# Keys and queries, and gates and first products, through joint scratch tensors and joint loads; another rhythm of the odd operand sums; seven more filler matmuls at the start

## The chip, the cores and the metric

One core of a Trainium2 chip runs the kernel. The time is the device time of one execution in microseconds (us), as the median of several. The engines are PE (matmul), PEld (PE's weight loads), DVE (VectorE), ACT (ScalarE), POOL (GpSimd) and SP (SyncE, which here only issues transfers). SPq and ACTq are the rows in which SP and ACT issue transfers.

## The reference, cut to what matters

A residual block over x of 2048 rows by 1024 columns, in float32:

```
h      = rms_norm(x) * (1 + scale(c)) + shift(c)
x_rnn, z_rnn, q, k, v, z_attn, g_r, g_a = split(h @ W_in)          # 8 x 1024 columns
y_rnn  = (rg_lru(conv(x_rnn)) * silu(z_rnn)) @ w_out_rnn
y_attn = (mixture over windows 128/1, 512/4, 2048/16 of attention(rope(q), rope(k), v)
          * silu(z_attn)) @ w_out_attn                              # 8 heads of 128
merged = sigmoid(g_r + bg_r) * y_rnn + sigmoid(g_a + bg_a) * y_attn
out    = rms_norm(x + gate(c) * (merged @ w_o))
```

The keys and values of the three windows are taken at strides 1, 4 and 16.

## The kernel before, in words

Every float32 operand is split in a high part of type fp32r (on ACT, line 159) and a low remainder (on DVE, line 168, or POOL, line 165). A product is then three matmuls for each 128 rows of its contraction (mm3, line 151), each with a 128x512 moving operand. The 2048 rows are four banks of 512 columns once transposed; the kernel's first half (f = 0) treats banks 0 and 1, its second half (f = 1) banks 2 and 3.

**The start** (lines 640 to 830). The modulation by c is computed column by column: sums on DVE (`sums`, line 669), column sums over the partitions on PE (`columns`, one-column matmuls into V), `modulation` on DVE (L692, L693), and then `build_x`, which makes the operand of a 128-row block k: ACT writes its high part T (L570) and a full copy hf (L573), DVE the remainder (L168). The first products X, Z, W, V need it. ACT also splits the raw weights, S<-R (`hi_k`, L159), which come by transfer as R<-in_w_in; these splits stand in ACT's order between the builds. Between the column sums PE runs filler matmuls (`idle_matmuls`, lines 625 to 633: bf16, 128x512, into a tile that nobody reads); their counts stand in lines 768 to 779 as written out by hand.

**The input projection** multiplies 2x2 blocks of operands by sums and differences of weights, seven products for eight (a Strassen form). The operands of an odd bank and the sums T1 to T4 are made by the generator `build_odd` (line 592): four yields build the odd bank's blocks (hx), then eight more parts, two for each k, make the sums. A part takes DVE operations L609 to L619 and, for each result, a split: T<-hx or T<-t on ACT, the remainder on DVE. `values_half` (line 877) says when each part is issued beside the value products: "free" (its operations take their place in the order as they come), "tied" (`tc.issue_after(last_ev[0])`: behind the last eviction so far), or one by one beside the last four quarter products. The eviction of a value product is ACT's ev<-X (L855), after which PE may write that bank again.

**Scratch.** Queries and keys are written transposed to DRAM tensors qT and kT, for each class c (row number modulo 4) 512 columns of 128 per bank. The gates of the two branches are in grT and gaT, the first projection's gated result in mrT.

**Attention and the output projections** run together from about 1340 us on: the head's work in units, and between them steps of `steps` (line 1723), a generator that runs the two projections pj = y @ w tile by tile, 128 rows of the output by one bank, eight k of three matmuls each, 24 matmuls a tile. Jobs 0 to 3 are y_rnn by bank (yaT), jobs 4 to 7 y_attn (oT). Tile t loads its weights (`load_w`, L339 for S<-wD, L1740 for S<-wR and st<-wR late), its gates (`load_g`, L1778, into tiles fg of four buffers), multiplies in `evict` (DVE, L1784; for oT also adds mrT's tile, L1786) and stores (L1792). Late in the kernel (from t = TAIL0 on, after the heads) the weights are split by ACT and DVE here: st and S.

A head's class c is loaded by `load_kq` (line 1426) into kraw: keys first, then the head's queries, two transfers (L1432, L1433), both on SP except class 3 of the first head, which goes by ACT's queue. `split_kq` makes KQ of it, and `window_queries`, `scores` and `keys` read columns of KQ. In the first half a class has 256 columns of keys, in the second 512, and 256 of queries.

SP's order is fixed by the program. A transfer holds one of eight semaphores in turn, and SP waits with the next one for the transfer eight before it; SP also waits for whatever the transfer reads or overwrites, and all behind it wait too. ACT, DVE and POOL are in order as well.

Of the kernel before, what the change touches and what calls it, by code (L numbers as in the profile page):

```python
# [90 lines left out]
def decoder_block(ctx, tc, x, c, positions, g_norm, w_mod, b_mod, w_in, b_gate, conv_w, conv_b,  # L91
# [21 lines left out]
    mrT = scratch("mrT", [D, S])  # L113
    oT = scratch("oT", [D, S])
    meT = scratch("meT", [D, S])
    gateD = scratch("gateD", [1, D])
# [585 lines left out]
    with tc.manual_schedule():  # L702
# [78 lines left out]
        products(0)  # L781
        sums(1, 1)
# [337 lines left out]
    plain_at = [None]  # L1120
    pu = [None]
    NT0, NT1 = (4, 5), 3
    QK = ((2 * D, qT, -SCALE), (3 * D, kT, 1.0))

    def scaled(t, ps, u, qs):

# [8 lines left out]

    def rotated_pairs(qp, f, Ct, St):

        for base, dstT, qs in QK:
            def rotated(i, j, ps, u, dstT=dstT, qs=qs):
                n = 2 * f + j  # L1140
                cq = slice(j * CH, (j + 1) * CH)
                t0 = T(qp, [P, CH], F32, "t0", bufs=NT0[f])
                scaled(t0, ps, u, qs)
                v = []

                def shuffle():
                    v.append(T(qp, [P, CH], F32, "t1", bufs=NT1))
                    nc.vector.stream_shuffle(v[0][:], t0[:], swap)
                    nc.gpsimd.tensor_tensor(t0[:], t0[:], Ct[:, cq], ALU.mult)

                def sines():
                    nc.vector.tensor_tensor(v[0][:], v[0][:], St[:, cq], ALU.mult)

                def add():
                    nc.vector.tensor_tensor(v[0][:], v[0][:], t0[:], ALU.add)

                def store():
                    for hh in range(4):
                        r0 = (4 * i + hh) * P
                        nc.sync.dma_start(dstT[r0 : r0 + 32, :, n * P : (n + 1) * P],  # L1160
                                          v[0][hh * 32 : (hh + 1) * 32, :].rearrange("p (r j) -> p r j", r=4))
# [18 lines left out]

    def plain_pairs(f):

        for base, dstT, qs in QK:
            for t in range(0, 6, 2):
                def plain(i, j, ps, u, t=t, dstT=dstT, qs=qs):
                    n = 2 * f + j
                    t0 = plain_at[0]()
                    wait = scaled(t0, ps, u, qs)

                    def store():  # L1190
                        for p0, r0, m in cuts[t + i]:
                            nc.sync.dma_start(dstT[r0 : r0 + m, :, n * P : (n + 1) * P],
                                              t0[p0 : p0 + m, :].rearrange("p (r j) -> p r j", r=4))
# [226 lines left out]
    class Head:  # L1420
        def __init__(self, f, h):
            self.f, self.h, self.bk = f, h, banks(f)
            self.nk = (self.bk[1] + 1) * P
            self.Q1, self.V, self.V1, self.u, self.raw = {}, {}, {}, {}, {}


        def load_kq(self, c):
            rows = slice(self.h * P, (self.h + 1) * P)
            t = T(ap_, [P, KQW], F32, "kraw", bufs=4)
            q0 = self.bk[0] * P  # L1430
            queue = nc.scalar if self.f == self.h == 0 and c == 3 else nc.sync
            queue.dma_start(t[:, : self.nk], kT[rows, c, : self.nk])  # L1432
            queue.dma_start(t[:, self.nk : self.nk + 2 * P], qT[rows, c, q0 : q0 + 2 * P])  # L1433
            self.raw["kq", c] = t

        def split_kq(self, c):
# [4 lines left out]
        def window_queries(self, i):  # L1441

            t = T(ap_, [P, 2, 4, 4, 32], F32R, "q1")
            for l in range(2):
                src = KQ[:, l, :, self.nk + i * P : self.nk + (i + 1) * P].bitcast(F32)
                copy = nc.gpsimd if self.f or self.h else nc.vector
                copy.tensor_copy(t[:, l], src.rearrange("p r (b a) -> p b r a", b=4))
            self.Q1[i] = t[:].rearrange("p l b r a -> p l b (r a)")
# [45 lines left out]
        def scores_c(self, r):  # L1494
            tiles = []
            for i, n in enumerate(self.bk):
                w = (n + 1) * P
                if self.f or n == 0:
                    ps = T(sc, [P, CH], F32, "sc")
                o0 = P if n == 1 else 0  # L1500
                q = slice(self.nk + i * P, self.nk + (i + 1) * P)
                mm3(ps[:, o0 : o0 + w], KQ[:, 0, r, q], KQ[:, 1, r, q], KQ[:, 0, r, :w], KQ[:, 1, r, :w],
                    first=n != 1, last=True, skip_group_check=True)
                tiles.append((ps[:, o0 : o0 + w], w))

            def softmax():
                t = T(ap_, [P, 2 * CH], F32, "pp", bufs=NPP)
                pt = self.u["c", r] = []
                for i, (ps, w) in enumerate(tiles):
                    pp = t[:, i * CH : i * CH + w]  # L1510
                    self.softmax_tile(ps, m23[:, CH - w :], 0, r, i, pp)
                    pt.append(pp)
            return softmax

        def keys(self, l, w0, nb):

            ap = KQ[:, l, 0, w0 * 32 : w0 * 32 + 32]
# [205 lines left out]
    def steps(jobs):  # L1723

        tiles = [(j, m) for j in range(len(jobs)) for m in range(KT)]
        Y, G = {}, {}

        def load_w(x):

# [41 lines left out]
        def load_g(t):  # L1771
            j, m = tiles[t]
            w, ys, n = jobs[j]
            at_ = slice(m * P, (m + 1) * P), slice(n * CH, (n + 1) * CH)
            G[t] = []
            for src in (grT,) if ys is yaT else (gaT, mrT):
                g = T(fl, [P, CH], F32, "fg", bufs=4)
                nc.sync.dma_start(g[:], src[at_])  # L1778
                G[t].append(g)

        def evict(t, ps):
            g = G[t]
            o = T(pR, [P, CH], F32, f"R{t % 4}") if t >= TAIL0 else g[0]
            nc.vector.tensor_tensor(o[:], ps[:], g[0][:], ALU.mult)  # L1784
            if len(g) > 1:
                nc.vector.tensor_tensor(o[:], o[:], g[1][:], ALU.add)  # L1786
            g[0] = o

        def store(t):
            j, m = tiles[t]  # L1790
            w, ys, n = jobs[j]
            nc.sync.dma_start((mrT if ys is yaT else meT)[m * P : (m + 1) * P, n * CH : (n + 1) * CH], G.pop(t)[0][:])  # L1792

        for k in range(KT):
            split_y(0, k)
# [406 lines left out]
```

## Time and profile before

| | |
|---|---|
| median of three runs | 2179.32 us (2177.88 to 2179.99) |
| profiled execution | 2180.94 us, of it the span 2179.2 us |
| granted clock, mean | 0.997 |
| PE busy | 2145.1 us, 98% of the span |
| DVE, ACT, POOL busy | 68%, 60%, 49% |
| transfers | 522.98 MB, mean 240 GB/s |

The span goes from the first to the last instruction; 1.7 us of the execution lie around it. Rows of the timeline read: start, duration, engine, line, operation, result<-inputs, shape, count, and in brackets the idle time of the engine ahead of it with what ended it. Matmuls overlap: a row of twelve lasts 2.88 us, and the next may begin 2.72 us after it. A row of the waits reads: who waited for whom, us in all, times, longest. A row of the windows reads: stretch, its length, busy time and instructions of each engine, granted clock of PE (1.00 is full), DMA share, GB/s.

### The profile page before, as it was taken

The numbers are of one execution on the slowest core, as the hardware profiler recorded it, in microseconds if no ns is written. First come the engines' busy times: TensorE is split into PE (matmuls) and PEld (weight loads), VectorE is DVE, ScalarE is ACT, GpSimd is POOL, SyncE is SP. The second block draws the span as 40 slices with busy tenths as digits, with TensorE's granted clock in tenths as the row PEclk, the third lists the DMA queues.
The fourth block names the chain that finished last, engine by engine and source line by source line (L and its number), as shares of the span: only waits on it lengthen the run. The fifth ranks groups of instructions, "written<-read, shape, count | busy, mean of one in ns | idle before, by whom it ended". The sixth has DMA issues, their size and how long they took to land.

```text
span 2179.2 us, 32758 instructions
## 1 busy us (share of the span) xinstructions
PE 2145.1 (98%) x10564; PEld 1791.9 (82%) x10564; DVE 1483.5 (68%) x2564; ACT 1313.1 (60%) x2621; POOL 1075.2 (49%) x803
## 2 busy tenths in 40 slices
PE   9999999999999999999999999999999999999998
PEld 6878888888788888888888887888888988878886
DVE  6579877868656535545446584577777777688887
ACT  5648668668644537457447532677888887343333
POOL 1357677667666323223224665456666665200543
PEclk9999999999999999999999999999999999999999
DMA  8457887887655378899996666888887877898552
GB/s 302 141 202 255 281 299 270 288 287 240 174 112 164 110 247 284 291 312 310 322 330 214 164 160 194 287 251 253 279 262 222 259 236 239 291 314 296 179 174 107
DMA packets 426608, 522.98 MB, mean 240 GB/s; under 512 B 104166, under 2 KB 291778, under 8 KB 425412
## 3 DMA queue, kind: packets, MB, share of 16 engines
q1 hardware_dynamic: 391860, 421.06, 61.9%
q10 hardware_dynamic: 34384, 99.78, 12.3%
q8 instruction: 84, 1.38, 0.2%
q14 instruction: 88, 0.72, 0.1%
q0 software_dynamic: 192, 0.05, 0.0%
HBM read 332.02 MB, written 188.75 MB: 239 GB/s over the span
## 4 chain that ended last, share of the span: by engine, by line
PE 59%; DMA 6%; issue 2%; POOL 2%; ACT 2%; DVE 2%; SPq 1%; ACTq 0%; POOLq 0%; DVEq 0%
PE X L151 12%; PE V L151 11%; PE pj L151 10%; PE Z L151 6%; PE W L151 6%; PE Y L151 5%; PE o L151 3%; PE sc L151 3%; DMA S<-wD 1%; PE pg L151 1%; DMA kraw<-kT 1%; PE pT L1570 1%; DMA vraw<-vN 1%; PE pT L1583 1%; DMA R<-yaT 1%
## 5 line engine op out<-in xcount | busy, mean ns | idle before, releaser
L165 POOL TENSOR_TENSOR S<-R,S 128x512 fp32r<-128x512 f32 x192 | 293.2, 1535 | 182.6 <-ACT S L159 89.3
L151 PE MATMUL X<-T,S 128*128 128x512 f32 x1344 | 326.2, 392 | 4.7 <-ACT ev L855 3.6
L151 PE MATMUL pj<-yh,S 128*128 128x512 f32 x896 | 324.5, 403 | 2.3 <-DMA S<-wD 1.6
L151 PE MATMUL V<-T,S 128*128 128x512 f32 x1344 | 324.2, 390 | 0.2 <-DVE ev L454 0.2
L151 PEld LDWEIGHTS X<-T,S 128*128 128x128 f32 x1344 | 253.3, 189 | 59.2 <-ACT ev L855 4.0
L151 PEld LDWEIGHTS V<-T,S 128*128 128x128 f32 x1344 | 252.0, 188 | 53.8 <-DVE ev L454 0.7
L165 POOL TENSOR_TENSOR S<-s,S 128x512 fp32r<-128x512 f32 x116 | 172.2, 1484 | 144.9 <-ACT S L159 105.5
L151 PEld LDWEIGHTS pj<-yh,S 128*128 128x128 f32 x896 | 168.4, 188 | 32.6 <-DVE st L1485 2.0
L151 PE MATMUL pj<-yl,S 128*128 128x512 f32 x448 | 176.2, 393 | 1.9 <-POOL yl L165 1.4
L1486 ACT ACTIVATE pp<-pp,st 128x256 f32<-128x256 f32 (+3 forms) x256 | 133.5, 523 | 52.9 <-DVE st L1485 52.3
L159 ACT ACTIVATE S<-s 128x512 fp32r<-128x512 f32 x124 | 77.4, 624 | 142.7 <-DVE s L284 92.0
L151 PE MATMUL Z<-T,S 128*128 128x512 f32 x672 | 162.0, 390 | 0.0
L151 PE MATMUL Y<-T,S 128*128 128x512 f32 x672 | 161.8, 390 | 0.0
L151 PE MATMUL W<-T,S 128*128 128x512 f32 x672 | 161.6, 389 | 0.0
L159 ACT ACTIVATE S<-R 128x512 fp32r<-128x512 f32 x200 | 121.2, 621 | 60.1 <-issue 20.4
L168 DVE TENSOR_TENSOR ptl<-pT,pth 128x384 fp32r<-128x384 f32 (+1 forms) x160 | 97.8, 628 | 77.3 <-ACT pth L159 75.1
L151 PEld LDWEIGHTS W<-T,S 128*128 128x128 f32 x672 | 126.0, 188 | 26.9 <-issue 0.9
L151 PEld LDWEIGHTS Z<-T,S 128*128 128x128 f32 x672 | 126.1, 188 | 26.2
L151 PEld LDWEIGHTS Y<-T,S 128*128 128x128 f32 x672 | 125.9, 188 | 26.1
L974 DVE SCALAR_TENSOR_TENSOR xc<-xr,par,xc 128x512 f32<-128x512 f32 x96 | 103.6, 1079 | 54.9 <-ACT xc L968 52.7
L165 POOL TENSOR_TENSOR s<-R,s 128x512 fp32r<-128x512 f32 x32 | 44.1, 1378 | 187.8 <-ACT s L159 168.7
L1550 ACT ACTIVATE pp<-pp,M 128x256 f32<-128x256 f32 (+3 forms) x256 | 118.0, 523 | 9.6 <-DVE M L1673 9.6
(417 smaller groups left out, 4902.9 us busy)
## 6 DMA issues: line engine op xcount, KB each, us to landing
sD<-S ACTq DMA_DIRECT2D x140, 512.0 KB, 3.6
S<-sD SPq DMA_DIRECT2D x140, 512.0 KB, 5.0
S<-wD SPq DMA_DIRECT2D x82, 512.0 KB, 5.6
R<-in_w_in_dram SPq DMA_DIRECT2D x144, 256.0 KB, 3.6
wD<-s ACTq DMA_DIRECT2D x64, 256.0 KB, 5.1
T<-in_w_mod_dram SPq DMA_DIRECT2D x16, 512.0 KB, 8.9
vN<-ev SPq DMA_DIRECT2D x32, 256.0 KB, 2.7
zaT<-ev SPq DMA_DIRECT2D x32, 256.0 KB, 4.4
```

Source lines behind the costliest of these rows:

```text
L151: nc.tensor.matmul(o, lhsT=l, rhs=r, start=st, stop=sp, **kw)
L159: nc.scalar.activation(o, i, AF.Copy)
L165: nc.gpsimd.tensor_tensor(o, i, h.bitcast(F32), ALU.subtract)
L168: return nc.vector.tensor_tensor(o, i, h.bitcast(F32), ALU.subtract).ins
L974: nc.vector.scalar_tensor_tensor(xc, xr[:, i : i + CH], cw(i), xc, ALU.mult, ALU.add)
L1486: nc.scalar.activation(pdst, pdst, AF.Exp, bias=m_, scale=-1.0, accum_out=l_)
L1550: nc.scalar.activation(pp, pp, AF.Copy, scale=w)
L1570: nc.tensor.transpose(pt[:, c0 + j * P : c0 + (j + 1) * P], pp[i][:, k * P : (k + 1) * P], ident)
L1583: nc.tensor.transpose(pt[:, c * P : (c + 1) * P], pp[:, half * P : (half + 1) * P], ident)
```

## The change

Four things are changed.

1. qT and kT become one tensor kqT with the columns q0 q1 k0 k1 k2 k3 q2 q3 (numbers are banks), so that what a head needs of a class lies side by side in either half: 512 columns in the first, 768 in the second. `load_kq` makes one transfer of it, always on SP.
2. gaT and mrT become the two halves of gmT; an oT tile loads both with one transfer of 512 KB into a tile of two halves. A yaT tile loads its one gate into a half of such a tile, two tiles sharing one. There are two such tiles in place of four single ones.
3. At the start, filler matmuls: 4 for 2 ahead of `last_sums`, 2 for 1 inside it (twice), and 3 new ones behind `turn_x(1)`.
4. The eight parts of the odd sums are issued 2 free, 2 tied, 1, 1, 1, 1 instead of 1 free, 2 tied, 2, 1, 1, 1.

```
-    qT = scratch("qT", [D, 4, NB * P])
-    kT = scratch("kT", [D, 4, NB * P])
+    kqT = scratch("kqT", [D, 4, 2 * NB * P])
+    q_column = lambda n: (n if n < 2 else NB + n) * P
+    k_column = lambda n: (2 + n) * P
...
-    gaT = scratch("gaT", [D, S])
+    gmT = scratch("gmT", [2, D, S])
+    gaT, mrT = gmT[0], gmT[1]
...
-        idle_matmuls(2)
-        last_sums(0, fill=1)
+        idle_matmuls(4)
+        last_sums(0, fill=2)
         modulation(0)
         hi_k(1)
         sums(1, 2)
         build_x(0)
         lo_k(1)
         turn_x(1)
+        idle_matmuls(3)
...
         for x, _ in enumerate(wide_values(vx, 1, n1, (1, 0), ws)):
-            if x == 0:
+            if x < 2:
                 next(odd)
         with tc.issue_after(last_ev[0]):
             next(odd)
             next(odd)
-        for x, _ in enumerate(wide_values(vx, 0, n1, (0, 1))):
+        for _ in wide_values(vx, 0, n1, (0, 1)):
             next(odd, None)
-            if x == 0:
-                next(odd, None)
...
             self.nk = (self.bk[1] + 1) * P
+            self.q0, self.k0 = (self.nk, 0) if f else (0, 2 * P)
...
             t = T(ap_, [P, KQW], F32, "kraw", bufs=4)
-            q0 = self.bk[0] * P
-            queue = nc.scalar if self.f == self.h == 0 and c == 3 else nc.sync
-            queue.dma_start(t[:, : self.nk], kT[rows, c, : self.nk])
-            queue.dma_start(t[:, self.nk : self.nk + 2 * P], qT[rows, c, q0 : q0 + 2 * P])
+            c0, w = self.f * 2 * P, self.nk + 2 * P
+            nc.sync.dma_start(t[:, :w], kqT[rows, c, c0 : c0 + w])
...
-            G[t] = []
-            for src in (grT,) if ys is yaT else (gaT, mrT):
-                g = T(fl, [P, CH], F32, "fg", bufs=4)
-                nc.sync.dma_start(g[:], src[at_])
-                G[t].append(g)
+            if ys is yaT:
+                if t % 2 == 0:
+                    both[0] = T(fl, [P, 2, CH], F32, "fg", bufs=2)
+                g = both[0][:, t % 2]
+                nc.sync.dma_start(g, grT[at_])
+                G[t] = [g]
+            else:
+                g = T(fl, [P, 2, CH], F32, "fg", bufs=2)
+                nc.sync.dma_start(g[:], gmT[:, at_[0], at_[1]].rearrange("g p c -> p g c"))
+                G[t] = [g[:, 0], g[:, 1]]
```

The rest of the diff gives the stores, the slices of KQ and the operands of `evict` their new places. Behind lines 100 and 780 the line numbers shift by one, in the later parts by a few; L159 becomes L160, L168 L169, L855 L857, L339 L340, L1778 L1779 and L1783.

**ACT, the last splits and evictions of the values of the first half.** T<-hx and T<-t are splits of the odd sums, S<-R and S<-s splits of the next weights, ev the evictions of the value products W, X, V, X; sD<-S are stores issued by ACT. Before:

```order
L159 ACTIVATE T_894<-t_197_1115 128x512
L159 ACTIVATE S_228_1262<-R_218_1236 128x512
L159 ACTIVATE S_226_1256<-s_219_1238 128x512
L855 ACTIVATE ev_1178<-W_1024 128x512
L159 ACTIVATE T_888<-hx_687 128x512
L855 ACTIVATE ev_1187<-X_1025 128x512
L159 ACTIVATE T_890<-hx_691 128x512
L855 ACTIVATE ev_1196<-V_1026 128x512
L855 ACTIVATE ev_1205<-X_1027 128x512
L159 ACTIVATE T_894<-t_211_1211 128x512
```

After, at the same place:

```order
L160 ACTIVATE T_902<-t_198_1123 128x512
L279 DMA sD<-S_223_1254 128x1024
L160 ACTIVATE T_896<-hx_695 128x512
L160 ACTIVATE S_229_1270<-R_219_1244 128x512
L160 ACTIVATE S_227_1264<-s_220_1246 128x512
L160 ACTIVATE T_898<-hx_699 128x512
L857 ACTIVATE ev_1186<-W_1040 128x512
L857 ACTIVATE ev_1195<-X_1041 128x512
L160 ACTIVATE T_902<-t_212_1219 128x512
L857 ACTIVATE ev_1204<-V_1042 128x512
```

Both T<-hx stand ahead of W's eviction now, and T<-t ahead of V's; before, each eviction had one split less ahead of it.

**DVE, the operations that these splits wait for.** hx_687 and hx_691 before are hx_695 and hx_699 after; L612 (L613 after) finishes the first, L615 (L616) the second. Before:

```order
L609 TENSOR_TENSOR t_206_1164<-hx_691,hx_687 128x512
L168 TENSOR_TENSOR T_889<-hx_686,T_888 128x512
L619 TENSOR_TENSOR t_197_1115<-t_197_1115,T_141 128x512
L168 TENSOR_TENSOR T_891<-hx_690,T_890 128x512
L611 TENSOR_TENSOR hx_687<-hx_687,T_138 128x512
L297 TENSOR_TENSOR s_220_1239<-R_218_1236,s_220_1239 128x512
L168 TENSOR_TENSOR T_893<-t_206_1164,T_892 128x512
L168 TENSOR_TENSOR T_895<-t_197_1115,T_894 128x512
L612 TENSOR_TENSOR hx_687<-hx_687,T_139 128x512
L615 TENSOR_TENSOR hx_691<-hx_691,hx_687 128x512
L168 TENSOR_TENSOR T_889<-hx_687,T_888 128x512
```

After:

```order
L610 TENSOR_TENSOR t_207_1172<-hx_699,hx_695 128x512
L169 TENSOR_TENSOR T_899<-hx_698,T_898 128x512
L620 TENSOR_TENSOR t_198_1123<-t_198_1123,T_141 128x512
L612 TENSOR_TENSOR hx_695<-hx_695,T_138 128x512
L169 TENSOR_TENSOR T_901<-t_207_1172,T_900 128x512
L613 TENSOR_TENSOR hx_695<-hx_695,T_139 128x512
L169 TENSOR_TENSOR T_903<-t_198_1123,T_902 128x512
L298 TENSOR_TENSOR s_221_1247<-R_219_1244,s_221_1247 128x512
L616 TENSOR_TENSOR hx_699<-hx_699,hx_695 128x512
L169 TENSOR_TENSOR T_897<-hx_695,T_896 128x512
```

Between L609 and L615 stood eight operations, now seven; and counted from DVE's wait for the first split behind the wide weights (the row at 105.67 us in the trace before), L612 was the 25th operation, and L616 is now the 23rd, since three operations have moved ahead of that wait.

**SP, the first tiles of attention.** kraw are the keys and queries, S<-wD the projection's weights, fg its gates. Before (the fourth pair is on ACT's queue):

```order
L1778 DMA fg_12115<-grT 128x512
L1395 DMA msk_12080<-in_cst_dram 128x896
L1432 DMA kraw_12128<-kT 128x256
L1433 DMA kraw_12128<-qT 128x256
L1432 DMA kraw_12131<-kT 128x256
L1433 DMA kraw_12131<-qT 128x256
L1432 DMA kraw_12134<-kT 128x256
L1433 DMA kraw_12134<-qT 128x256
L339 DMA S_2258_12149<-wD 128x1024
L339 DMA S_2260_12168<-wD 128x1024
L1778 DMA fg_12179<-grT 128x512
```

After:

```order
L1395 DMA msk_12088<-in_cst_dram 128x896
L1432 DMA kraw_12136<-kqT 128x512
L1432 DMA kraw_12138<-kqT 128x512
L1432 DMA kraw_12140<-kqT 128x512
L1432 DMA kraw_12142<-kqT 128x512
L340 DMA S_2259_12153<-wD 128x1024
L340 DMA S_2261_12172<-wD 128x1024
L1779 DMA fg_12123<-grT 128x512
```

Between the mask and the first weights stand four transfers in place of six. SP issues 1291 transfers and other listed rows in place of 1385: 62 fewer for keys and queries, 32 fewer for gates. Late in the kernel a tile's list loses one of five to seven, such as the second of `fg<-gaT`, `fg<-mrT`.

More of the change, by code (lines that the diff above doesn't have):

```diff
@@ L1122, in decoder_block @@
     NT0, NT1 = (4, 5), 3
-    QK = ((2 * D, qT, -SCALE), (3 * D, kT, 1.0))
+    QK = ((2 * D, q_column, -SCALE), (3 * D, k_column, 1.0))
     def scaled(t, ps, u, qs):
@@ L1136, in rotated_pairs, with rotated @@
     def rotated_pairs(qp, f, Ct, St):
-        for base, dstT, qs in QK:
-            def rotated(i, j, ps, u, dstT=dstT, qs=qs):
+        for base, column, qs in QK:
+            def rotated(i, j, ps, u, column=column, qs=qs):
                 n = 2 * f + j
@@ L1181, in plain_pairs, with plain @@
     def plain_pairs(f):
-        for base, dstT, qs in QK:
+        for base, column, qs in QK:
             for t in range(0, 6, 2):
-                def plain(i, j, ps, u, t=t, dstT=dstT, qs=qs):
+                def plain(i, j, ps, u, t=t, column=column, qs=qs):
                     n = 2 * f + j
@@ L1444, in window_queries @@
             for l in range(2):
-                src = KQ[:, l, :, self.nk + i * P : self.nk + (i + 1) * P].bitcast(F32)
+                src = KQ[:, l, :, self.q0 + i * P : self.q0 + (i + 1) * P].bitcast(F32)
                 copy = nc.gpsimd if self.f or self.h else nc.vector
@@ L1500, in scores_c @@
                 o0 = P if n == 1 else 0
-                q = slice(self.nk + i * P, self.nk + (i + 1) * P)
-                mm3(ps[:, o0 : o0 + w], KQ[:, 0, r, q], KQ[:, 1, r, q], KQ[:, 0, r, :w], KQ[:, 1, r, :w],
+                q = slice(self.q0 + i * P, self.q0 + (i + 1) * P)
+                ks = slice(self.k0, self.k0 + w)
+                mm3(ps[:, o0 : o0 + w], KQ[:, 0, r, q], KQ[:, 1, r, q], KQ[:, 0, r, ks], KQ[:, 1, r, ks],
                     first=n != 1, last=True, skip_group_check=True)
@@ L1515, in keys @@
         def keys(self, l, w0, nb):
-            ap = KQ[:, l, 0, w0 * 32 : w0 * 32 + 32]
+            ap = KQ[:, l, 0, self.k0 + w0 * 32 : self.k0 + w0 * 32 + 32]
             return bass.AP(ap.tensor, ap.offset, [list(ap.ap[0]), [32, nb], [KQW, 4], [1, 32]])
@@ L1725, in steps @@
         tiles = [(j, m) for j in range(len(jobs)) for m in range(KT)]
-        Y, G = {}, {}
+        Y, G, both = {}, {}, [None]
         def load_w(x):
@@ L1774, in load_g @@
             at_ = slice(m * P, (m + 1) * P), slice(n * CH, (n + 1) * CH)
-            G[t] = []
-            for src in (grT,) if ys is yaT else (gaT, mrT):
-                g = T(fl, [P, CH], F32, "fg", bufs=4)
-                nc.sync.dma_start(g[:], src[at_])
-                G[t].append(g)
+            if ys is yaT:
[8 more added lines that the diff above has]
+                G[t] = [g[:, 0], g[:, 1]]
         def evict(t, ps):
             g = G[t]
-            o = T(pR, [P, CH], F32, f"R{t % 4}") if t >= TAIL0 else g[0]
-            nc.vector.tensor_tensor(o[:], ps[:], g[0][:], ALU.mult)
+            o = T(pR, [P, CH], F32, f"R{t % 4}")[:] if t >= TAIL0 else g[0]
+            nc.vector.tensor_tensor(o, ps[:], g[0], ALU.mult)
             if len(g) > 1:
-                nc.vector.tensor_tensor(o[:], o[:], g[1][:], ALU.add)
+                nc.vector.tensor_tensor(o, o, g[1], ALU.add)
             g[0] = o
@@ L1791, in store @@
             w, ys, n = jobs[j]
-            nc.sync.dma_start((mrT if ys is yaT else meT)[m * P : (m + 1) * P, n * CH : (n + 1) * CH], G.pop(t)[0][:])
+            nc.sync.dma_start((mrT if ys is yaT else meT)[m * P : (m + 1) * P, n * CH : (n + 1) * CH], G.pop(t)[0])
         for k in range(KT):
```

5 lines of the change are left out of this document (2 added, 3 removed).

## The prediction

> **What bounds the kernel now.** I read the page first, then the table of windows, then PE's waits stage by stage, and last the rows of single engines around those waits.
>
> ```profile
> span 2179.2 us, 32758 instructions
> PE 2145.1 (98%) x10564; PEld 1791.9 (82%) x10564; DVE 1483.5 (68%) x2564; ACT 1313.1 (60%) x2621; POOL 1075.2 (49%) x803
> ...
> 0.00:60.00 60.00, 56.29 (x280) 40.60 (x280) 37.41 (x86) 34.84 (x56) 9.93 (x16) 0.97 0.87 293
> 110.00:230.00 120.00, 116.41 (x502) 95.65 (x501) 101.64 (x110) 76.12 (x125) 80.25 (x52) 0.97 0.69 238
> 1340.00:1500.00 160.00, 154.49 (x950) 133.84 (x950) 95.83 (x318) 111.99 (x349) 85.85 (x85) 1.00 0.86 267
> 1880.00:2020.00 140.00, 136.80 (x599) 111.70 (x598) 113.51 (x181) 57.00 (x100) 5.15 (x4) 1.00 0.90 303
> ```
>
> PE is busy for 2145.1 of 2179.2 us, and the change leaves every product where it is. So the only time to win is PE's 34.1 idle us and what PE loses at half clock. The windows' columns are length, then busy time of PE, PE's weight loads, DVE, ACT and POOL, then granted clock, DMA share and GB/s. The four stages where the edits change most hold 3.71, 3.59, 5.51 and 3.20 idle us, 16.0 together, under half of the 34.1; apart from the clock, more than that is not to be won there.
>
> **The start: seven more idle matmuls.** Three windows show the two places where the clock is down.
>
> ```profile
> 17.15:20.56 3.41, 2.42 (x17) 2.03 (x18) 2.25 (x6) 1.43 (x3) 0.00 (x0) 1.00 1.10 348
> 20.56:23.98 3.42, 3.42 (x10) 2.68 (x9) 3.38 (x7) 1.99 (x4) 0.00 (x0) 0.50 1.08 363
> ...
> 126.38:133.20 6.82, 5.43 (x13) 4.28 (x14) 5.88 (x7) 3.94 (x8) 3.00 (x2) 0.50 0.43 138
> ```
>
> From 20.56 to 23.98 PE runs at 0.50 and is busy all the time, so it does 1.71 us of work in 3.42: the dip costs 1.7 us of PE time. The window ahead of it is busy for 2.42 of 3.41 us, and the seven extra matmuls fall just there. I expect that they keep the clock up. Whether PE's 1.7 us reach the end is read from who waits next:
>
> ```profile
> 17.49 0.58 PE L151 MATMUL V<-ones,acc 128*128 128x1 f32 x4 [0.42 <-DVE acc L669]
> 19.96 0.73 PE L151 MATMUL X<-S,T 128*128 128x512 f32 x2 [0.65 <-ACT T L570]
> ...
> 34.30 0.50 PE L151 MATMUL X<-S,T 128*128 128x512 f32 x1 [0.32 <-DVE T L168]
> 39.61 0.73 PE L151 MATMUL X<-S,T 128*128 128x512 f32 x2 [0.31 <-ACT T L570]
> ...
> 31.55 0.63 ACT L159 ACTIVATE S<-R 128x512 fp32r<-128x512 f32 x1 [0.88 <-DMA R<-in_w_in_dram]
> 38.26 0.63 ACT L159 ACTIVATE S<-R 128x512 fp32r<-128x512 f32 x1 [4.74 <-DMA R<-in_w_in_dram]
> 38.80 0.76 ACT L570 ACTIVATE T<-pg,mod,gs 128x512 fp32r<-128x512 f32 x1
> ```
>
> ACT works in order. At 38.26 its split S<-R has waited 4.74 us for a transfer, the operand T that PE wants at 39.61 is built behind it, and the same holds at 31.55 for the product at 34.30. The transfer does not depend on PE (DMA share 0.87 over the stage), so a PE that comes 1.7 us sooner waits 1.7 us longer. On the cost side, seven matmuls at 0.227 us (twelve take 2.72 us: 135.90 to 138.62 in rows below) are 1.6 us, against 0.42 + 0.65 us of waits in which they fit; the other 0.5 us delays PE by as much, and the same cover takes that. **Value 0, bounds −1.7 and +0.5.**
>
> [...]
>
> **The odd sums, first half.** ACT's order changes most at the end of the values stage.
>
> ```profile
> 105.67 0.69 DVE L168 TENSOR_TENSOR T<-hx,T 128x512 fp32r<-128x512 f32 x1 [19.04 <-ACT T L159]
> 106.28 0.68 DVE L168 TENSOR_TENSOR T<-t,T 128x512 fp32r<-128x512 f32 x1
> ...
> 117.93 1.78 DVE L612 TENSOR_TENSOR hx<-hx,T 128x512 f32<-128x512 f32 x1
> ...
> 125.89 0.68 DVE L612 TENSOR_TENSOR hx<-hx,T 128x512 f32<-128x512 f32 x1
> 126.61 1.64 DVE L615 TENSOR_TENSOR hx<-hx,hx 128x512 f32<-128x512 f32 x1
> ...
> 126.60 0.63 ACT L159 ACTIVATE T<-hx 128x512 fp32r<-128x512 f32 x1 [1.46 <-DVE hx L612]
> 127.14 0.58 ACT L855 ACTIVATE ev<-X 128x512 f32<-128x512 f32 x1
> ...
> 127.77 5.49 PE L151 MATMUL X<-T,S 128*128 128x512 f32 x12 [3.59 <-ACT ev L855]
> ...
> 135.90 2.88 PE L151 MATMUL W<-T,S 128*128 128x512 f32 x12
> 138.62 2.88 PE L151 MATMUL V<-T,S 128*128 128x512 f32 x12
> ```
>
> PE stands for 3.59 us until ACT has evicted bank X at 127.72. That eviction is queued on ACT behind the split T<-hx, which waits for DVE's L612, the 25th DVE operation after DVE's own wait at 105.67. With the change, three DVE operations have been done before that wait, but both evictions (W and X) are queued behind a split that waits for L615, one operation further: the 23rd. Two operations fewer at 0.61 us (105.67 to 106.28) are 1.2 us: L615 ends near 125.4. Then ACT does the split (0.54), W's eviction (about 0.54, formerly ahead of the wait) and X's (0.58): X is free at 127.0 instead of 127.72. **Value −0.7.** DVE operations take 1.78 instead of 0.68 us where POOL works beside them; if the two that go are slow ones (1.7 each) the gain is 2.9, and if two more become slow it is a loss of 1.5: bounds −2.9 and +1.5. V's eviction moves behind a split that waits for L619, but PE asks for V only at 138.62.
>
> The stall is also why the clock falls again: 6.82 us at 0.50 with 5.43 busy, a loss of 2.7 us. 2.9 idle us are hardly less than 3.6, so I keep this loss: **value 0**, bounds 0 and −1.7 (one of the two 3.41 us windows goes).
>
> **Attention, its first tiles.** Two loads per class become one, and the pair on ACT's queue comes to SP.
>
> ```profile
> 1354.41 0.32 SPq L1433 DMA_DIRECT2D kraw<-qT  x1
> 1356.36 0.80 SPq L339 DMA_DIRECT2D S<-wD  x2
> ...
> 1358.14 0.85 PE L151 MATMUL sc<-kq 128*128 128x128 f32 x5 [0.40 <-DVE kq L168]
> 1361.97 0.47 PE L151 MATMUL pj<-yh,S 128*128 128x512 f32 x1 [1.59 <-DMA S<-wD]
> 1362.74 1.46 PE L151 MATMUL sc<-kq,q 128*128 128x128 f32 x11
> ...
> 1360.86 0.75 DVE L1447 CAST q<-kq 128x512 fp32r<-128x512 f32 x2
> ```
>
> The weights S<-wD go out at 1356.36, as the ninth transfer counted from fg (the order is shown with the change), 5.6 us ahead of PE's restart at 1361.97. With two fewer ahead of it (six kraw loads become four) it goes out where a kraw load now stands, near 1354.4, lands near 1360.0, and PE's 1.59 us go. What is late next is DVE's pair of casts, which end at 1361.6: PE then wants q at 1362.74 − 1.59 = 1361.15, and of the saving up to 0.45 us comes back; I give back 0.3. **Value −1.3, bounds 0 and −2.0** (both waits).
>
> **The rest of attention.** The 62 saved issues help PE only where it waits for what hangs on a load.
>
> ```profile
> PE sc L151 <- DVE st L1485: 2.3, 3, 1.7
> ...
> PE sc L151 <- POOL q L1447: 1.3, 2, 0.8
> PE pj L151 <- POOL yl L165: 0.8, 2, 0.6
> ```
>
> From 1365 to 1880 no wait of PE is for a DMA. 2.1 us are for POOL, whose copies follow the kraw loads; I take a quarter, **−0.5**, bounds −2.1 and +2.1 (as much the other way, since one load of twice the size lands as a whole). A yaT tile still takes one gate load, so there the pair tile changes little.
>
> **The second projection's gates.** One load of 512 KB takes the place of two of 256 KB, 32 times.
>
> ```profile
> PE pj L151 <- DVE st L168: 1.8, 2, 1.4
> PE pj L151 <- DVE yl L168: 0.7, 1, 0.7
> ...
> 1925.35 0.69 DVE L1784 TENSOR_TENSOR R<-pj,fg 128x512 f32<-128x512 f32 x1 [2.19 <-DMA fg<-gaT]
> 1926.88 0.69 DVE L1786 TENSOR_TENSOR R<-R,fg 128x512 f32<-128x512 f32 x1 [0.84 <-DMA fg<-mrT]
> ...
> 1928.83 0.73 PE L151 MATMUL pj<-yh,st 128*128 128x512 f32 x2 [1.35 <-DVE st L168]
> ```
>
> DVE waits for both halves, and the weights' remainder (st) and the operands (yl) stand behind in its queue; PE waits 1.35 us for them. In this stretch a tile of 24 matmuls (5.44 us) goes with up to seven transfers. One fewer is 5.44/7 = 0.8 us per tile, 1.6 over the two tiles that a load is ahead. That covers most of DVE's 2.19 and, through it, PE's 1.35. **Value −1.4**, bounds −3.2 (all idle time of this window) and +1.5: the multiply now waits for both halves, and the second came 1.53 us after the first (1925.35 to 1926.88).
>
> **Sum.** 0 − 0.7 + 0 − 1.3 − 0.5 − 1.4 = −3.9 us. The profiled execution took 2180.94 us (span 2179.2 and 1.7 around it), so it would take 2177.0. The median shown, 2179.32, is 1.6 below the profiled execution; beside that median I forecast **2175.4**.
>
> **Rivals.**
> - *The clock comes through.* The first dip's 1.7 us is not absorbed, or the second loses one of its windows (1.7): both give 2175.4 − 3.4 = 2172.0. For it speaks that PE is 98% busy; against it ACT's 4.74 us behind a transfer. Chance 0.22.
> - *Transfers, not issues, are the limit.* With DMA share 0.86 to 0.90, fewer and larger loads land when the small ones did; the terms of attention and gates (3.2) vanish: 2178.6, no change. Against it: SP's S<-wD stands behind others at 1356.36. Chance 0.20.
> - *Slower: the whole pair is late.* The multiply starts with the second half. At 1926.88 both operations would then still be to do, where now only the addition is: DVE's queue moves back by one operation, 0.6 us, and by whatever the joint load lands later than the second half did. At 0.7 us in each of the twelve tiles (5.44 us each) from 1880 to 1945, DVE's remainders reach PE 12 × 0.7 = 8.4 us late: 2175.4 + 1.4 + 8.4 = 2185.2. From 0.2 us per tile it undoes the forecast's gain, from 0.6 it makes the kernel slower by over 0.2%. Against it: PE waits for DVE just 2.5 us there in all. Chance 0.13.
> - *The forecast*: 0.45, its own range 2173 to 2177.5.
>
> **How the numbers follow.** A measurement of this kernel tells 0.2% (4.4 us) from no change, so faster means below 2175.0. The forecast lies on that line: 0.24 faster and 0.21 same; with the rivals, faster 0.46, same 0.41, slower 0.13. The range reaches down to 2172.0 with the odd sums' and the gates' far ends partly added (−3.5), 2168.5, and up to 2178.6 with two bounds of +1.5: 2181.6. Some 0.18 lie outside.
>
> **What would show it.** Start: no window at 0.50 near 20, and longer waits of PE near 34 and 39; if PE there runs on without them, the first rival is right. Odd sums: X's first product after the stall near 127.1. Attention: S<-wD issued near 1354.4 and no DMA wait of PE near 1362. Gates: DVE's wait near 1925 under 1 us, and one fg row per tile. A stall of PE in a new place would make the sum wrong.

## The result and the profile after

| | before | after |
|---|---|---|
| median of seven runs | 2179.32 us (2177.88 to 2181.4) | 2186.7 us (2184.11 to 2190.08) |
| ratio, 95% interval | 1 | 1.0032 (1.002 to 1.0044) |
| profiled execution | 2180.94 us | 2190.08 us, the slowest of its seven |

The change made the kernel slower by 7.4 us, where 3.9 faster was forecast; the time lies 5 us above the range. The page after, then its table of windows (length, busy time of PE, PEld, DVE, ACT, POOL, granted clock, DMA share, GB/s):

```profile
span 2188.3 us, 32588 instructions
PE 2149.3 (98%) x10570; PEld 1792.0 (82%) x10571; DVE 1482.1 (68%) x2564; ACT 1313.3 (60%) x2621; POOL 1073.3 (49%) x803
...
0.00:60.00 60.00, 56.61 (x283) 40.87 (x285) 37.38 (x86) 34.48 (x56) 9.93 (x16) 0.97 0.87 291
110.00:230.00 120.00, 116.59 (x505) 95.51 (x504) 97.62 (x106) 73.63 (x121) 81.44 (x53) 0.99 0.68 235
230.00:560.00 330.00, 327.66 (x1444) 268.67 (x1443) 263.44 (x278) 234.27 (x379) 232.91 (x157) 1.00 0.79 269
1340.00:1500.00 160.00, 155.53 (x952) 134.82 (x951) 95.46 (x317) 110.93 (x345) 84.70 (x84) 1.00 0.86 270
1880.00:2020.00 140.00, 131.75 (x562) 105.37 (x561) 108.09 (x172) 54.33 (x94) 3.59 (x3) 0.99 0.92 298
```

Of the four stages only the last is much worse: 8.25 idle us of PE instead of 3.20. It is clearer still when each matmul of PE is found in both traces and its start in the one subtracted from its start in the other (a few matmuls that a trace lacks are skipped). This lag of the kernel after, in us:

| at (before) | 20 | 60 | 122 | 142 | 223 | 406 | 566 | 706 | 1353 | 1373 | 1875 | 1895 | 1935 | 1996 |
|---|---|---|---|---|---|---|---|---|---|---|---|---|---|---|
| lag | 0.5 | 0.5 | 0.5 | -0.6 | -0.3 | 2.5 | 3.1 | 3.0 | 2.5 | 1.1 | 0.9 | 4.9 | 8.3 | 9.1 |

The 1.1 us gained between 122 and 142 are the clock's: after PE's stall near 127 us it stays at 0.50 for one window of 3.41 us (129.16 to 132.57), and in the kernel before for two (126.38 to 133.20). Part 4 alone is at 0.9998 of before (below), so this is not shown to be a gain of part 4 either.

Attention's start gives 1.4 back. From 1875 to 1996, where the second projection runs alone, 8.2 us are lost. The trace of before is no fixed mark there: of the kernels below, the four with the single gate tiles of before gain 0.4 to 2.9 us on it, so the loss is rather larger than smaller. The 2.8 us between 223 and 406 belong to no edit that the runs show: in the windows PE's idle time from 230 to 560 is 2.34 us, where before has 0.59, and 1.6 us of it are three waits for ACT's evictions in the input projection; in the other kernels' traces the lag grows there too, by 0.5 to 1.4 us, and in the one with the first products loaded first (below) by 2.7. The traced execution is the slowest of its seven.

SP's transfers at the place of the loss, first of before, then of after. fg<-gaT, fg<-mrT and fg<-gmT are gates and first products, meT<-fg the stores of products that stand in a gate's tile, S<-wR weights:

```profile
1878.72 0.43 SPq L1778 DMA_DIRECT2D fg<-gaT  x1
1879.24 0.75 SPq L1740 DMA_DIRECT2D S<-wR  x1
1880.04 0.74 SPq L1792 DMA_DIRECT2D meT<-fg  x1
1883.58 0.32 SPq L1778 DMA_DIRECT2D fg<-mrT  x1
1884.01 0.36 SPq L1740 DMA_DIRECT2D S<-wR  x1
```

```profile
1879.72 0.32 SPq L1740 DMA_DIRECT2D S<-wR  x1
1880.14 1.28 SPq L1797 DMA_DIRECT2D meT<-fg  x1
1886.90 0.37 SPq L1783 DMA_DIRECT2D fg<-gmT  x1
1887.33 0.46 SPq L1740 DMA_DIRECT2D S<-wR  x1
...
1891.18 0.46 SPq L1797 DMA_DIRECT2D meT<-fg  x1
1896.13 0.37 SPq L1783 DMA_DIRECT2D fg<-gmT  x1
```

Before, the gates of the first late tile (t = 40) go out at 1878.72, ahead of the store of tile 38, since a tile of first products is free as soon as it has been added. After, the pair tile of tile 38 is free only when the store of its first half has landed: 1880.14 issued, the load behind it at 1886.90, and the weights behind that at 1887.33 instead of 1884.01. Before, the transfer ahead of those weights, fg<-mrT at 1883.58, stood 1.9 us for the first products of tile 39 to land and 0.8 us for DVE's sum with them, and for no store; after, the load stands 5.4 us for the store (the longest of each row, from SP's waits of 1872 to 1950):

```profile
SPq L1778 <- DMA fg<-mrT: 2.6, 2, 1.9
...
SPq L1778 <- DVE fg L1786: 0.8, 1, 0.8
```

```profile
SPq L1783 <- DMA meT<-fg: 6.1, 2, 5.4
```

What it does to PE and DVE:

```profile
1894.11 0.80 PE L152 MATMUL pj<-yh,S 128*128 128x512 f32 x1 [2.88 <-ACT S L160]
1894.70 0.63 PE L152 MATMUL pj<-yl,S 128*128 128x512 f32 x1
1895.13 1.05 PE L152 MATMUL pj<-yh,S 128*128 128x512 f32 x2
```

```profile
1894.69 0.68 DVE L1789 TENSOR_TENSOR R<-pj,fg 128x512 f32<-128x512 f32 x1
...
1902.66 0.69 DVE L1789 TENSOR_TENSOR R<-pj,fg 128x512 f32<-128x512 f32 x1 [3.39 <-DMA fg<-gmT]
```

PE waits 2.88 us for ACT's split of those weights, and starts again at 0.43 us per matmul (1894.70 to 1895.13): the clock has fallen, for 3.41 us at 0.50 (1893.85 to 1897.26), which is 1.7 us of PE's work. The next gates (1896.13) wait for the sum of tile 40, and DVE then waits 3.39 us for them.

### The profile page after: what moved, and what is told of

Its sections match the earlier page's. It is cut to its first block, busy times and chain, and to the rows that moved or that the text cites. A ratio compares the mean times of both kernels' runs of the same rounds, so it can differ in the third digit from the quotient of the medians.

```text
span 2188.3 us, 32588 instructions
## 1 busy us (share of the span) xinstructions
PE 2149.3 (98%) x10570; PEld 1792.0 (82%) x10571; DVE 1482.1 (68%) x2564; ACT 1313.3 (60%) x2621; POOL 1073.3 (49%) x803
## 4 chain that ended last, share of the span: by engine, by line
PE 60%; DMA 5%; POOL 2%; DVE 2%; issue 2%; ACT 2%; SPq 1%; ACTq 0%; POOLq 0%; DVEq 0%
PE X L152 12%; PE V L152 11%; PE pj L152 9%; PE Z L152 6%; PE W L152 6%; PE Y L152 5%; PE sc L152 4%; PE o L152 4%; PE pg L152 1%; PE pT L1570 1%; PE pT L1583 1%; DMA kraw<-kqT 1%; POOL yl L166 1%; DMA S<-wR 1%; DMA fg<-gmT 1%
## 5 line engine op out<-in xcount | busy, mean ns | idle before, releaser
L160 ACT ACTIVATE S<-s 128x512 fp32r<-128x512 f32 x124 | 77.4, 624 | 146.2 <-DVE s L285 89.1
L160 ACT ACTIVATE S<-R 128x512 fp32r<-128x512 f32 x200 | 121.4, 622 | 61.6 <-issue 17.2
L169 DVE TENSOR_TENSOR ptl<-pT,pth 128x384 fp32r<-128x384 f32 (+1 forms) x160 | 97.9, 629 | 77.2 <-ACT pth L160 75.0
```

The lines of the kernel that those rows point to most:

```text
L160: nc.scalar.activation(o, i, AF.Copy)
L169: return nc.vector.tensor_tensor(o, i, h.bitcast(F32), ALU.subtract).ins
```

## The experiments

Theory A: the loss is the pair tile's, which is held by a store. Theory B: it is the joint load's, for all of which the multiply waits. Theory C: it lies in the other parts. Medians are of 5 to 11 runs; each ratio is to runs of before on the same chip (medians 2179.99 to 2180.61).

**Part 2 alone, and part 2 undone.** Before with joint tensor, pair tiles and joint load; and the kernel after with single tiles again (the joint tensor stays). Of the second edit:

```
...
-                g = T(fl, [P, 2, CH], F32, "fg", bufs=2)
-                nc.sync.dma_start(g[:], gmT[:, at_[0], at_[1]].rearrange("g p c -> p g c"))
-                G[t] = [g[:, 0], g[:, 1]]
+            for src in (grT,) if ys is yaT else (gaT, mrT):
+                g = T(fl, [P, CH], F32, "fg", bufs=4)
+                nc.sync.dma_start(g[:], src[at_])
...
```

> The kernel before with part 2 alone (joint tensor, pair tiles and one load of 512 KB). Theory A and B: the loss of the second projection alone, 7.3 us, 2186 us (2184 to 2188). Theory C: 2178 to 2180.

> The kernel after, with the gates and first products of an oT tile loaded by two transfers into two of four single tiles again (part 2 of the change undone; the joint scratch tensor stays). Theory A, the pair tile is held until the store of the product that stands in its first half has landed, so the load for the first late tile blocks SP's queue ahead of the weights: the 7.3 us lost between 1875 and 1940 go, near 2179.5 us (2177.5 to 2182). Theory B, a joint load of 512 KB lands later as a whole and the multiply waits for it in many tiles: the same 2179.5. Theory C, the loss lies in other parts (start, odd sums, what follows them from 230 to 560 us): it stays at 2185 to 2188.

Part 2 alone: 2189.2 us, 1.0042 (1.0028 to 1.0055). Without it: 2178.8, 0.9994 (0.9986 to 1.0003). Theory C falls: part 2 costs 9.0 us in one comparison and 7.9 in the other (8.7, if each of the two kernels is taken against the runs of before beside it), and all else is near nothing.

**Two loads into the pair tile** (the tile is still one buffer):

```
-                nc.sync.dma_start(g[:], gmT[:, at_[0], at_[1]].rearrange("g p c -> p g c"))
+                for i in range(2):
+                    nc.sync.dma_start(g[:, i], gmT[i, at_[0], at_[1]])
```

> The kernel after, with the two halves of the pair tile loaded by two transfers of 256 KB each; the tile is still one buffer. Theory A (held buffer): nothing is won, 2185 to 2189 us, and the load for the first late tile still waits some 6 us for a store. Theory B (joint load lands late): the loss goes, 2179 to 2181. Theory C: 2185 to 2188, with no stall of PE near 1890.

2183.17 us, 1.0015 (1.0006 to 1.0024), between the two theories: 3.5 us of the loss go, and PE's stall near 1890 stays, 2.9 us in this trace too. So both seem to be at work; the square below shows it.

**The first late load two steps later.**

```
-                    if k == 0 and t == TAIL0:
+                    if k == 2 and t == TAIL0:
```

> The kernel after, with the gates of the first late tile (t = TAIL0) loaded at its third step instead of its first, so that on SP three transfers of weights stand ahead of that load instead of behind it. Theory A: the weights no longer wait behind the held buffer, PE's 2.9 us wait near 1890 and the clock's fall after it go; 3 to 5 us are won, 2181.5 to 2184 us. Theory B: nothing changes, 2185 to 2188. Theory C: nothing changes.

2185.82 us, 1.0027 (1.0016 to 1.0038): hardly anything. The single stall of 2.9 us near 1890 is indeed gone (the lag grows by only 0.6 us from 1884 to 1893), but the wait went elsewhere, to DVE, and by 1902 the lag has grown by 5.6 us more; the clock falls here too (mean 0.94 from 1892 to 1904 and 0.97 from 1904 to 1940). DVE's rows in this kernel:

```profile
1892.66 0.69 DVE L1789 TENSOR_TENSOR R<-pj,fg 128x512 f32<-128x512 f32 x1 [4.24 <-DMA fg<-gmT]
...
1900.81 0.69 DVE L1789 TENSOR_TENSOR R<-pj,fg 128x512 f32<-128x512 f32 x1 [3.69 <-DMA fg<-gmT]
```

By the program the load still starts only when the store has landed; now the weights are early and the gates late.

**Tiles of their own for t = 40 and 41**, in columns of an operand tile that is empty then, with the joint load and with two:

```
-                g = T(fl, [P, 2, CH], F32, "fg", bufs=2)
+                if TAIL0 <= t < TAIL0 + 2:
+                    g = B["T4"][t % 2][:, 2:4, :].bitcast(F32)
+                else:
+                    g = T(fl, [P, 2, CH], F32, "fg", bufs=2)
```

> The kernel after, with the joint load of 512 KB kept, but the gates of the first two late tiles (t = 40 and 41) put into parts of operand tiles that are not yet in use, so that no load waits for a store or for the sum of the tile before it. Theory A (held pair tile alone): the whole loss of the second projection goes, 2177.5 to 2180.5 us beside 2180 of before. Theory B (a joint load lands later as a whole, in every late tile): about half of it stays, as the kernel with two loads into the pair tile suggests (it kept 3.7 of 7.3): 2182 to 2184.5 us. Had both nothing to do with it: 2186.

> As the kernel with own tiles for t = 40 and 41, and besides two loads of 256 KB for each pair tile instead of one. Theory A: no gain over the joint load, 2177.5 to 2180.5 us. Theory B: 2178 to 2180.5, some 3 us under the kernel with own tiles and joint loads.

2182.29 us, 1.001 (1.0001 to 1.0018), and 2178.38 us, 0.9988 (0.998 to 0.9997). With the two kernels above they make a square:

| us | joint load | two loads |
|---|---|---|
| pair tile held by the store | 2186.7 | 2183.17 |
| own tiles for t = 40, 41 | 2182.29 | 2178.38 |

The held tile costs 4.4 or 4.8 us, the joint load 3.5 or 3.9. The four kernels did not all run beside the same runs of before; against those beside each, the square is 7.4 and 3.0 us in the first row, 1.7 and -2.2 in the second. Then the held tile costs 5.2 or 5.7 us and the joint load 3.9 or 4.4. The two add up, and both theories hold; which share is larger is not settled by intervals of some 2 us either way on each of the four. The last kernel is the only one here whose interval lies wholly below before, by 1.2 thousandths; two close relatives of it (below) are at 0.9993 and 1.0, so a gain over before is not shown. From issue to landing (last column, median us, transfers of 1880 to 2000) in the kernel after, the one with two loads, the one with own tiles, and the one with own tiles and two loads:

```profile
fg<-gmT SPq DMA_DIRECT2D x20, 512.0 KB, 7.8
```

```profile
fg<-gmT SPq DMA_DIRECT2D x42, 256.0 KB, 5.2
```

```profile
fg<-gmT SPq DMA_DIRECT2D x20, 512.0 KB, 7.1
```

```profile
fg<-gmT SPq DMA_DIRECT2D x40, 256.0 KB, 5.6
```

And the waits for gates from 1876 to 2000, first with own tiles and the joint load (9.9 us in all), then with own tiles and two loads (6.5):

```profile
DVE R L1792 <- DMA fg<-gmT: 5.1, 4, 1.5
DVE fg L1792 <- DMA fg<-gmT: 3.4, 1, 3.4
DVE R L1792 <- DMA T4l<-gmT: 1.4, 1, 1.4
```

```profile
DVE fg L1793 <- DMA fg<-gmT: 2.0, 1, 2.0
DVE R L1793 <- DMA fg<-gmT: 1.9, 1, 1.9
DVE R L1793 <- DMA T4l<-gmT: 1.7, 1, 1.7
DVE R L1795 <- DMA fg<-gmT: 0.3, 2, 0.2
DVE R L1795 <- DMA T4l<-gmT: 0.3, 1, 0.3
DVE fg L1795 <- DMA fg<-gmT: 0.3, 1, 0.3
```

**The gates earlier**, at the fourth step of the tile before instead of its eighth, with both kinds of load:

```
+                    if k == 3 and t + 1 < len(tiles):
+                        load_g(t + 1)
                     if k == 7:
                         store(t - 1)
-                        if t + 1 < len(tiles):
-                            load_g(t + 1)
```

> The kernel with own tiles for t = 40 and 41 and joint loads, with the gates of tile t+1 now loaded at the fourth step of tile t instead of its eighth (2.7 us earlier, right after the sum of tile t-1 has set the pair tile free). If the joint load costs because it lands 7.1 us after its issue and the multiply waits for all of it (theory B): the 3.9 us between it and the kernel with two loads go, 2178 to 2179.5 us. If it costs by something that an earlier issue doesn't cure (transfers that share the engines with the weights): it stays at 2181.5 to 2183.

> The kernel with own tiles and two loads per pair tile, the gates likewise loaded 2.7 us earlier. Theory B: DVE hardly waits for them already (some 4 us in the late tiles), so little is won: 2177 to 2178.5 us beside 2178.4 without the earlier load.

2182.55 us, 1.0008 (0.9999 to 1.0017), and 2179.63, 1.0 (0.9991 to 1.0009): no gain, the second rather worse. The first stayed where the expectation put a cost that an earlier issue doesn't cure, but the edit moved more than the issue, so it settled nothing about the joint load: by the program the earlier load waits on SP for the sum of the tile before, and the weights behind it come later. ACT's wait for them, with own tiles, then with own tiles and earlier gates:

```profile
ACT S L160 <- DMA S<-wR: 28.3, 10, 5.0
```

```profile
ACT S L160 <- DMA S<-wR: 40.0, 16, 6.0
```

**What of the joint load costs.** Two loads with the order of the halves turned round (`for i in (1, 0)`), and two loads of 64 partitions of both halves:

> The kernel with own tiles and two loads per pair tile, with the first products loaded ahead of the gates, so that the multiply, which needs the gates, waits for the second load. If the joint load costs because the multiply waits for both halves: 2180.5 to 2182.5 us, most of the 3.9 us back. If it costs by its size: 2178 to 2179.3 us, as with the gates first.

> The kernel with own tiles and two loads per pair tile, each load with 64 partitions of both halves instead of one half on 128. If waiting for both halves is the cost: 2180.5 to 2182.5 us. If the size of one transfer is: 2178 to 2179.3 us. [...]

The first took 2180.74 us, 1.0001 (0.9992 to 1.001): 2.4 of the 3.9 us are back (2.9, each against before of its own runs). DVE's waits for gates are those of the joint load again (5.3, 3.2 and 1.8, 10.3 us in all):

```profile
DVE R L1793 <- DMA fg<-gmT: 5.3, 4, 2.2
DVE fg L1793 <- DMA fg<-gmT: 3.2, 1, 3.2
...
DVE R L1793 <- DMA T4l<-gmT: 1.8, 1, 1.8
```

So most of theory B is that the multiply has to wait for the half that it doesn't need. The rest, 1.1 to 1.5 us, can't be told from nothing by these intervals. The loads by partitions took 2186.96 us, 1.003 (1.0019 to 1.0042): 256 KB from 64 partitions landed after 7.1 us instead of 5.6, which hides what it was to show. Nor can its 8.6 us over the kernel with own tiles and two loads be laid to the gates' landing alone: the joint load into own tiles landed after 7.1 us too and cost 3.9, and in this kernel the weights S<-wR landed later as well (6.9 us instead of 5.5), with a DMA share, summed over the queues, of 1.03 from 1880 to 2000 instead of 0.96.

**The other parts alone.**

> Part 1 alone: keys and queries in one tensor and one load per class, the gates as before (single tiles, two loads), start and odd sums as before. By the prediction's term of -1.3 us: 2178 to 2179.5 us beside 2180 of before, PE's wait for S<-wD near 1362 gone and the lag of PE behind the kernel before falling by 1 to 1.7 us between 1350 and 1370. If loads and not issues were the limit: 2180 and no such step.

> Part 3 alone: the seven filler matmuls. By the prediction: 2179.5 to 2180.5 us, no difference; the clock may or may not fall near 20 us, and whatever PE wins there is gone by 40 us, behind the splits that wait for R<-in_w_in. By the rival (the clock's 1.7 us come through): 2178.3.

> Part 4 alone: the odd sums as two free, two tied and four single parts. By the prediction: 0.7 us faster, 2179.9 us beside 2180.6 of before, X's first matmul after the stall near 127.1 us. If POOL's remainder, which takes 5.30 instead of 1.55 us beside the DVE operations that now follow without a pause, is what ACT then waits for: no difference, 2180 to 2181, and X's first matmul at 127.7 to 127.9 us.

> The kernel with own tiles and two loads per pair tile, with start and odd sums as in the kernel before (parts 3 and 4 undone). If parts 3 and 4 are worth nothing, as the traces suggest (what the start wins is gone by 40 us; PE's wait near 127 us is 3.4 to 3.6 us with and without part 4): 2178.4 within 1 us. By the prediction's -0.7 for part 4: 0.7 us more than with it, 2179.1.

Keys and queries: 2179.03 us, 0.9993 (0.9984 to 1.0002). Start: 2180.36, 1.0001 (0.9992 to 1.001). Odd sums: 2179.25, 0.9998 (0.9989 to 1.0007). The best kernel without parts 3 and 4: 2178.39, as with them. None can be told from no change by itself.

## Why the prediction was wrong

**The start: right.** Part 3 alone is worth nothing. In that kernel the clock stays at 1.00 where the kernel before had 0.50 (20.56 to 23.98); its lag falls by 1.6 us from 20 to 24 us and is back by 34, so the 1.7 us are won and not kept, and the first rival falls as far as it rests on this dip. Waits that take them back lie somewhat earlier than forecast: two near 27 and 30 us (0.51 and 0.30), and one at the product of 34.30 (0.67 us instead of 0.32), while the one near 39 is unchanged (0.31). That the fillers keep the clock up is not shown: the kernel after has the same seven, and in its trace the clock fell. The window of part 3 alone, and its row:

```profile
20.56:23.98 3.42, 3.42 (x18) 2.82 (x17) 3.27 (x6) 1.61 (x3) 0.00 (x0) 1.00 1.08 364
```

```profile
34.46 0.50 PE L151 MATMUL X<-S,T 128*128 128x512 f32 x1 [0.67 <-DVE T L168]
```

By 102 us its lag behind the kernel before is 0.2. In the kernel after it fell for one window at another place. That left nothing either: the lag is 0.5 us at 20 us, ahead of it, 1.5 at 32, and 0.5 again at 40. Its window:

```profile
30.17:33.58 3.41, 3.41 (x9) 2.66 (x9) 2.71 (x4) 2.09 (x4) 0.00 (x0) 0.50 1.10 349
```

**The odd sums: wrong, by the whole 0.7 us.** PE's wait near 127 us is 3.4 to 3.7 us in every trace, with part 4 and without. The step that failed is that two DVE operations fewer bring the eviction forward by their time. In the kernel after, POOL, ACT and PE:

```profile
117.89 5.30 POOL L166 TENSOR_TENSOR S<-R,S 128x512 fp32r<-128x512 f32 x1 [4.22 <-DVE t L619]
123.15 1.29 POOL L166 TENSOR_TENSOR S<-s,S 128x512 fp32r<-128x512 f32 x1
```

```profile
124.47 0.34 ACTq L279 DMA_DIRECT2D sD<-S  x1
124.86 0.63 ACT L160 ACTIVATE T<-hx 128x512 fp32r<-128x512 f32 x1 [4.56 <-POOL S L166]
...
127.44 0.58 ACT L857 ACTIVATE ev<-X 128x512 f32<-128x512 f32 x1
```

```profile
128.07 2.49 PE L152 MATMUL X<-T,S 128*128 128x512 f32 x7 [3.37 <-ACT ev L857]
```

In the kernel before, the same POOL operation:

```profile
115.91 1.55 POOL L165 TENSOR_TENSOR S<-R,S 128x512 fp32r<-128x512 f32 x1 [3.16 <-ACT S L159]
```

DVE's chain does run ahead, without a pause until 122.04, and POOL beside it takes 5.30 us instead of 1.55. ACT's store sD<-S waits for POOL until 124.47, and the split and both evictions stand behind it. DVE itself waits for the POOL operation behind the long one (S<-s, until 124.44), ahead of the L616 that the prediction counted to:

```profile
124.47 0.69 DVE L298 TENSOR_TENSOR s<-R,s 128x512 f32<-128x512 f32 x1 [2.43 <-POOL S L166]
```

So L616 ends at 125.76, near the 125.4 of the prediction, but ACT still has two splits of weights ahead of T<-hx, and bank X is free at 128.02 instead of 127.0. The prediction let POOL slow DVE, not DVE slow POOL, and passed over the store in ACT's queue, which the order shown with the change has in its second row. The clock's term (0, bounds 0 and -1.7) came out as a gain of 1.1 us between 122 and 142: the clock was at 0.50 for one step of 3.41 us and not two, after a stall of 3.37 us instead of 3.59. The part alone shows the same POOL operation:

```profile
118.04 5.30 POOL L165 TENSOR_TENSOR S<-R,S 128x512 fp32r<-128x512 f32 x1 [4.83 <-DVE t L618]
```

**Attention's first tiles: the mechanism right, the size unsure.** With part 1, S<-wD goes out 4.0 us after the first kraw load instead of 6.3 (in part 1 alone 1350.78 and 1354.81; before 1350.08 and 1356.36), and PE's lag falls by 1.0 to 2.0 us between 1340 and 1400 in twelve traces with it, some 1.5 in the mean. But it falls by 0.4, 0.5 and 1.5 in three without it (0.6 in the mean, with the kernel before itself as 0): the 1.59 us of before is no fixed price. In the kernel with part 3 alone that wait is 0.3, and in one of the twelve with part 1 (the best kernel without parts 3 and 4) it is still 1.0:

```profile
PE pj L151 <- DMA S<-wD: 0.3, 1, 0.3
```

The forecast -1.3 is some -0.9 by these means of single traces. What is late next was named rightly: in the kernel after PE waits there for DVE's casts.

```profile
1363.05 0.47 PE L152 MATMUL pj<-yh,S 128*128 128x512 f32 x1 [0.97 <-DVE q L1446]
```

**The rest of attention:** from 1373 to 1875 the lag goes from 1.1 to 0.9, within the bounds, and -0.2 in place of -0.5.

**The gates: wrong in sign and far out of its bounds.** In place of -1.4 (-3.2 to +1.5) part 2 costs 8 to 9 us. Two steps failed. First, the prediction counted transfers and not what sets a tile free. It noted two pair tiles in place of four single ones, and that the yaT tiles change little, but not that before TAIL0 the product stays in its gate's tile until its store has landed, so that the first products' tile, free at once before, is now held with it: 4.4 to 5.7 us, with the fall of the clock that follows the stall (3.41 us at 0.50). This is the stall in a new place that the prediction named as a sign against its sum. Second, "one fewer is 0.8 us per tile" took a transfer of 512 KB as one like the others. It lands after 7.1 to 7.8 us instead of 5.2 to 5.6, and that wait for the second half was priced at +1.5 us in all as a bound; it is 3.5 to 4.4. Nor was there a fixed 3.2 us to win: PE's idle time from 1880 to 2020 is 0.72 us with part 3 alone and 1.03 with part 1 alone, where gates and their loads are as before. The slower rival had the place and the sign and, by chance, the size (2185.2); of its mechanism, the wait for both halves in many tiles, the runs show half, and the other half is one that the prediction didn't see.

## What to carry to other kernels

When two buffers are made one, look for the time at which each half became free before: the pair is free at the later of the two, and a load behind it in an in-order queue takes everything behind it along (here a load stood 5.4 us for a store, and the weights behind it went out at 1887.33 instead of 1884.01). A joint load saves an issue and delays the first use by the landing of the whole (7.1 to 7.8 us here, 5.2 to 5.6 for a half); where all of it is needed at once it cost nothing here (keys and queries, 0.9993 of before, within the noise), where the first half is needed first it cost some 4 us. Where engines wait in turn, a chain made shorter on one engine is worth what its neighbours leave (here nothing of 0.7 us): ask which operation runs beside it, and what stands in the queue between. And a wait of one trace is no fixed price (PE's for S<-wD was 1.59 us before and 0.3 with part 3 alone, which doesn't touch it): see whether it stands in several traces before it goes into a sum.

## What the hardware showed that was not expected

A POOL operation of 128x512 took 5.30 us instead of 1.55 (117.89 to 123.19) while DVE ran operations of 0.68 us without a pause beside it, while in the kernel before DVE's took 1.78 us at 117.93 beside POOL's of 1.74. So beside each other now the one took longer and now the other. In the seven traces with part 4 where POOL's rows were read it is 5.30 or 5.31 us, and the next one 1.28 or 1.29. In the kernel after it ends 1.15 us after the last of the unbroken row of DVE operations (122.04), so by these times it outlasted the whole row; what holds it the traces do not show.

The clock's fall at the start does not go by the number of fillers alone: with the start of before it fell at 20.56 us in the kernel before; with the seven filler matmuls it fell at 30.17 in the kernel after, and with part 3 alone the granted clock is 1.00 from 0 to 60.

Within each of the traces before and after, the changes of the clock between 20 and 2170 us lie whole steps of 3.41 us apart (before 20.56, 23.98, 126.38 and 133.20, after 30.17, 33.58, 129.16, 132.57, 1893.85 and 1897.26). In the step ahead of a fall PE was busy for 2.42 and 1.22 us before, and for 2.64, 1.09 and 0.79 after. In the one step at 0.50 after which the clock stayed down (126.38 to 129.79, before) PE was busy for 2.02 us; in the five after which it rose, for 3.15 to 3.42. Busy time alone does not tell the steps apart, though: in the kernel after PE was busy for 2.37 us from 122.33 to 125.74, less than in two of the steps ahead of a fall, and the clock stayed at 1.00 for one step more.
